# A hybrid decoder layer: x read in order of time and permuted out of PSUM, the constants read first, B and C turned on TensorE, states permuted back by ScalarE

## The chip, the core and the metric

The kernel runs on one core of one Trainium2 chip. The metric is the device time of one execution in microseconds (us), less is better. The kernel before took 3020.07 us, the median of three runs (3012.84 to 3021.89). The profiled execution is a fourth one and took 3016.45 us.

The engines are TensorE (PE; PEld are its weight loads), VectorE (DVE), ScalarE (ACT), GpSimd (POOL) and SyncE (SP). SP computes nothing here: its queue issues every DMA, in one order. Each engine works through its own queue in the order in which the program was built, and waits at an instruction until the semaphores that it names are there.

## What is computed

One layer over 2048 tokens of 1024 channels, all in float32:

```
h    = rmsnorm(x, norm_mix);  u, z, xbc, dt = split(h @ w_in)
y_a  = s5(u)      # 64 groups of 16 channels, each a complex diagonal
                  # state of 64:  s[t] = abar * s[t-1] + Bbar u[t]
                  # y = Re(C s) + d * u, then gelu and a gate
y_b  = mamba2(z, conv4(xbc), dt)       # 16 heads, chunks of 128
x    = x + concat(rmsnorm(y_a), rmsnorm(y_b)) @ w_out
out  = rmsnorm(x + swiglu_ffn(rmsnorm(x)))
```

S5 takes eight steps of time at once. With 256 such blocks, u of a group is a matrix of 128 rows (8 steps j by 16 channels) and 256 columns. A table M1 turns a block into what it adds to the state, the scan runs over the blocks, and two tables M2 and Q give the output: `y = M2' u + Q' state`. All three are made on the chip from lambda, the step, B and C.

## The kernel before

**Projection.** x is read in blocks of 512 tokens (four chunks of 128). `load_block` reads a chunk, squares it on ACT for the norm's sum, computes the scale on DVE and multiplies. `transposed_split` transposes the block on TensorE, 128 by 128, into PSUM tiles `ps_t`, and splits each into a rounded high part (ACT) and a rest (DVE). `project_pairs` takes two tiles of 128 output columns at a time: `split_w` reads the weights (`wst`), rounds them on ACT (`whi`), takes the rest on POOL (`wlo`), and each half block of 512 tokens then needs 24 matmuls into `ps_in` (lines 81 to 83). The first half of the tokens goes through u, then the convolved columns, then z; of the second half, two u tiles are made before the scan, and the rest beside it and after it. The convolution runs on DVE (`acc`, three products a tile).

**Order of time.** The columns that S5 and the convolution want are not in order of time. Token t of a chunk is `8*c + j`, and they want j outermost, c inside. `rows` does this in the load of x: it reads eight sets of sixteen rows, each row eight tokens after the one before. The projected columns then come out as (chunk k, j, c). What is written at the end goes back through `rows`.

**The start.** SP's queue holds the four chunks of block 0, then the constants `cm` (identity, triangles), eight small vectors, two weight tiles, and block 1. `s5_tables` then reads lambda, B with its states on the partitions (pieces of 16 elements), and C in tiles `ct` of 128 rows, eight of which are transposed on TensorE (`ps_c`) for each of two arrangements; seven DMAs from `zt` fill the upper part of M2's table with zeros. For each of eight sets of groups DVE makes W and Q (`W`, six products), TensorE transposes W (`ps_m`) and computes `ps_k`.

**The scan.** `s5_inputs` computes `ps_x` for eight groups and ACT copies it into X, as (block's m, s). `s5_scan` runs 15 steps of four DVE operations over m, a scan over the 16 s, and then adds the carried states to X with products `f1` and `f2` (two buffers under one tag `f`). The result XG lies as (m, s), and the matmul `ps_y` with Q reads it with a step of 16 elements, as (s, m).

**The other mixer.** `ssd_pair` handles two heads in 64 columns each; its product `ps_yd` takes the four chunks of the first head, then those of the second.

**What sets the order.** The program is written without semaphores. A scheduler with a model of time puts each engine's instructions in order, and ends of tiles in pools set when buffers come free: five slots of 16 KB (`take`, `slot`), two buffers for `wst`, `whi` and `wlo`, two for the conv's `xp`, one for `acc`. `issue_after` holds instructions behind a given one.

Of the kernel before, what the change touches and what calls it, by code (L numbers as in the profile page):

```python
# [112 lines left out]
def transposed_split(k, xb, gcol, hi, lo, wide=None):  # L113
# [16 lines left out]
    for kk in range(KD):  # L130
# [7 lines left out]
        k.evac = nc.scalar.activation(hi[:, kk, :], ps, AF.Identity, scale=g)  # L138
        nc.vector.scalar_tensor_tensor(lo[:, kk, :], ps, g, hi[:, kk, :].bitcast(F32), op0=MUL, op1=SUB)
# [132 lines left out]
def s5_tables(k, sp):  # L272
# [145 lines left out]
    for dst, (u0, u1) in ((c1_, (k.c_re, k.c_im)), (c2_, (k.c_im, k.c_re))):  # L418
        ct = sp.tile([P, 8, P], F32, name="ct", tag="M1", bufs=1)
        nc.sync.dma_start(ct[:, :, 0:64], u0.rearrange("(t a) h p -> (a h) t p", a=8))  # L420
        nc.sync.dma_start(ct[:, :, 64:128], u1.rearrange("(t a) h p -> (a h) t p", a=8))
        for q in range(2):
            ps = k.ps_x.tile([P, 512], F32, tag="x", name="ps_c")
# [1105 lines left out]
```

## Time and profile before

| | us |
|---|---|
| median of three runs | 3020.07 |
| the profiled execution | 3016.45 |
| its span on the core | 3014.7 |
| first projection matmul (L81) | 28.86 |
| first `ps_dt` matmul, which follows the u projection | 157.93 |
| first `ps_x` matmul of the scan | 454.66 |
| first `ps_w` matmul of the output projection | 1286.85 |

A window gives the busy time of each engine between two times, and the clock that TensorE was granted (1.00 is full). A wait gives who stood still and for whose result; a row of the timeline gives start, length, engine, line, operation, output and inputs. Matmul records overlap, so that the pace of a run of them is its length divided by their number, not the length of one record. A float32 matmul that is not rounded to fp32r counts as two records.

### The profile page before, as it was taken

To read this page: it belongs to the slowest core of one execution; us is meant where nothing else is said; L and a number is where in the kernel's file an instruction comes from. 1 tells how busy PE (TensorE), PEld (TensorE's weight loads), DVE (VectorE), ACT (ScalarE), POOL (GpSimd) and SP (SyncE) were. 2 spreads that over 40 slices of the span, in tenths; PEclk is the share of its full clock that TensorE was granted. 3 is DMA by queue.
4 is the path that set the end of the run, shared out by engine and by line. 5 is a ranking of instruction groups with operands and counts; after the bars stand their busy time and mean duration, and the time that the engine had idled before them with its cause. 6 is when DMAs were issued, how large, how long until landed. Compare 5 with 4: busy or idle time off the path is not lost.

```text
span 3014.7 us, 35741 instructions
## 1 busy us (share of the span) xinstructions
PE 2833.0 (94%) x12972; PEld 2257.6 (75%) x12972; DVE 2102.2 (70%) x3953; ACT 1118.2 (37%) x1817; POOL 535.6 (18%) x462
## 2 busy tenths in 40 slices
PE   4898999999999989989899999999999999999996
PEld 3776777677787777768677788887788887878875
DVE  5586218989668888797878755556655557677686
ACT  3134322333454333332434433334333334243343
POOL 1343311114366766510000000000000000000000
PEclk8999999999999999999999999999999999999998
DMA  6455335443446454545455222233222224545444
GB/s 118 116 157 169 117 97 173 140 140 104 132 129 191 145 165 140 174 153 172 134 167 161 74 75 82 84 112 101 96 84 84 79 76 141 194 168 192 165 153 140
DMA packets 331992, 398.84 MB, mean 132 GB/s; under 512 B 49804, under 2 KB 249592, under 8 KB 331816
## 3 DMA queue, kind: packets, MB, share of 16 engines
q1 hardware_dynamic: 331816, 396.56, 42.1%
q8 instruction: 102, 1.67, 0.2%
q14 instruction: 74, 0.61, 0.1%
HBM read 264.39 MB, written 132.12 MB: 132 GB/s over the span
## 4 chain that ended last, share of the span: by engine, by line
PE 62%; DVE 19%; DMA 11%; issue 3%; ACT 2%; SPq 2%; POOL 1%; DVEq 0%; ACTq 0%; POOLq 0%
PE ps_w L1126 40%; PE ps_in L81 4%; PE ps_in L83 4%; PE ps_in L82 4%; DMA s<-ybD 2%; DVE s L947 2%; DVE acc L731 1%; DMA out_dram<-x 1%; PE ps_y L575 1%; DVE wS L947 1%; PE ps_glu L81 1%; PE ps_glu L82 1%; PE ps_glu L83 1%; DVE x L1132 1%; DVE s L1179 1%
## 5 line engine op out<-in xcount | busy, mean ns | idle before, releaser
L1126 PE MATMUL ps_w<-s,wS 128*128 128x512 f32 x3936 | 957.7, 397 | 39.0 <-DVE s L947 16.8
L1126 PEld LDWEIGHTS ps_w<-s,wS 128*128 128x128 f32 x3936 | 747.3, 191 | 213.9 <-DVE s L947 18.8
L1126 PE MATMUL ps_w<-s,wA 128*128 128x512 f32 x2952 | 731.4, 398 | 29.8 <-DVE x L1132 10.3
L1126 PEld LDWEIGHTS ps_w<-s,wA 128*128 128x128 f32 x2952 | 558.8, 190 | 167.7 <-DVE x L1132 12.1
L81 PE MATMUL ps_in<-s,whi 128*128 128x512 f32 x896 | 353.5, 395 | 9.1 <-ACT xp L718 9.0
L83 PE MATMUL ps_in<-s,wlo 128*128 128x512 f32 x896 | 351.8, 395 | 1.6 <-POOL wlo L69 1.6
L82 PE MATMUL ps_in<-s,whi 128*128 128x512 f32 x896 | 352.9, 394 | 0.0
L942 ACT CAST wS<-sum 128x512 fp32r<-128x512 f32 (+1 forms) x336 | 203.5, 611 | 396.7 <-PE ps_w L1126 195.6
L947 DVE TENSOR_TENSOR wS<-sum,wS 128x512 fp32r<-128x512 f32 (+1 forms) x336 | 225.5, 675 | 140.5 <-ACT wS L942 139.9
L69 POOL TENSOR_TENSOR wlo<-wst,whi 128x1024 fp32r<-128x1024 f32 x72 | 188.7, 2621 | 424.1 <-ACT whi L66 424.0
L942 ACT CAST wA<-s 128x512 fp32r<-128x512 f32 (+1 forms) x252 | 150.7, 610 | 242.0 <-PE ps_w L1126 162.1
L81 PEld LDWEIGHTS ps_in<-s,whi 128*128 128x128 f32 x896 | 169.4, 189 | 49.0 <-ACT xp L718 10.3
L83 PEld LDWEIGHTS ps_in<-s,wlo 128*128 128x128 f32 x896 | 169.4, 189 | 40.9 <-issue 3.1
L82 PEld LDWEIGHTS ps_in<-s,whi 128*128 128x128 f32 x896 | 169.4, 189 | 36.9 <-issue 2.3
L1132 DVE TENSOR_TENSOR gu<-ps_w,gu 128x512 f32<-128x512 f32 x134 | 92.5, 691 | 148.3 <-PE ps_w L1126 144.5
L803 POOL TENSOR_TENSOR s<-cm,dtas 128x512 fp32r<-128x512 f32 x128 | 161.8, 1292 | 76.0 <-PE ps_seg L804 76.0
L947 DVE TENSOR_TENSOR wA<-s,wA 128x512 fp32r<-128x512 f32 (+1 forms) x252 | 165.1, 671 | 3.2 <-ACT wA L942 3.2
L1132 DVE TENSOR_TENSOR x<-ps_w,x 128x512 f32<-128x512 f32 x160 | 108.7, 685 | 57.1 <-PE ps_w L1126 56.9
L731 DVE SCALAR_TENSOR_TENSOR acc<-xp,cols,acc 128x1024 f32<-128x1024 f32 x72 | 102.7, 1426 | 50.6 <-ACT acc L729 49.9
L66 ACT CAST whi<-wst 128x1024 fp32r<-128x1024 f32 x72 | 75.5, 1049 | 167.9 <-PE ps_in L82 99.8
L1137 ACT COPY gu<-ps_w 128x512 f32<-128x512 f32 x134 | 78.4, 586 | 141.7 <-PE ps_w L1126 141.4
L1139 DVE TENSOR_TENSOR x<-x,sg 128x512 f32<-128x512 f32 x125 | 85.0, 686 | 65.7 <-ACT sg L1137 38.5
(354 smaller groups left out, 3612.8 us busy)
## 6 DMA issues: line engine op xcount, KB each, us to landing
wst<-in_w_in_dram SPq DMA_DIRECT2D x56, 512.0 KB
s<-in_w_gate_dram SPq DMA_DIRECT2D x22, 1024.0 KB
s<-in_w_up_dram SPq DMA_DIRECT2D x22, 1024.0 KB
actD<-gu SPq DMA_DIRECT2D x44, 512.0 KB
s<-actD SPq DMA_DIRECT2D x16, 1024.0 KB
xD<-xo SPq DMA_DIRECT2D x24, 512.0 KB
uD<-ev SPq DMA_DIRECT2D x16, 512.0 KB
zD<-sz SPq DMA_DIRECT2D x32, 256.0 KB
```

Source lines behind the costliest of these rows:

```text
L69: eng.tensor_sub(lo, st, hi.bitcast(F32))
L81: nc.tensor.matmul(ps, wh[:, i, :], rh[:, i, :], start=(i == 0), stop=False)
L82: nc.tensor.matmul(ps, wh[:, i, :], rl[:, i, :], start=False, stop=False)
L83: last = nc.tensor.matmul(ps, wl[:, i, :], rh[:, i, :], start=False, stop=(i == n - 1))
L731: V.scalar_tensor_tensor(acc, tap(i), col(i), acc, op0=MUL, op1=ADD)
L803: G.tensor_mul(r, bc(k.tri.unsqueeze(1), [P, 4, P]), bc(part, [P, 4, P]))
L942: a = k.nc.scalar.copy(op[:, 0], raw)
L947: b = eng.tensor_sub(op[:, 1, part], raw[:, part], op[:, 0, part].bitcast(F32))
L1126: nc.tensor.matmul(ps, a[:, p, i, :], b[:, q, i, :], start=(root == name and i == 0 and p + q == 0), stop=(i == n - 1 and p == 1), skip_gr ...
L1132: V.tensor_add(dst, ps, dst if onto else src)
L1137: nc.scalar.copy(dst, bank[root])
L1139: V.tensor_add(block, block, dst)
```

## The change

There are six parts.

1. x of blocks 0 to 3 is read row by row. The permutation moves to the two operations that take `ps_t` out of PSUM: they read each eighth element. A block's columns are now (j, n) with 64 n, so that whoever takes `ps_in` out reads (j, k, c) and writes (k, j, c) as before (`chunks`, `by_chunk`).
2. `cm` is read first. The load of block 1 is issued after the first two weight tiles (`early`), and the second of these is no longer held behind the evacuation of block 0.
3. B and C are read raw, with the groups on 64 partitions, into slot 3, in six DMAs (B in rows of 4 KB, C in pieces of 256 B); `by_state` turns them with 64 transposes of 64 rows and eight ACT copies. Slot 3 held block 1 of x before.
4. The scan's last addition stays in f1, on all 128 partitions (before: two additions over 64 partitions each, straight into XG). ACT copies f1 into XG, four times a set, now as (s, m), so that the matmul with Q reads adjacent elements.
5. `ps_yd` alternates between the two heads.
6. The outputs of u are written as 8 runs of 64 instead of runs of 16.

```diff
@@ transposed_split
-        k.evac = nc.scalar.activation(hi[:, kk, :], ps, AF.Identity, scale=g)
-        nc.vector.scalar_tensor_tensor(lo[:, kk, :], ps, g, hi[:, kk, :].bitcast(F32), op0=MUL, op1=SUB)
+        view = lambda t: t[:, kk, :].rearrange("p (j n) -> p j n", j=8)
+        src = ps.rearrange("p (n j) -> p j n", j=8)
+        k.evac = nc.scalar.activation(view(hi), src, AF.Identity, scale=g)
+        nc.vector.scalar_tensor_tensor(view(lo), src, g, view(hi).bitcast(F32), op0=MUL, op1=SUB)
@@ fetch_block (new; load_block calls it or is given xb)
+        k.load = k.nc.sync.dma_start(xb[:, i, :], k.x[ch * P : ch * P + P, :])
@@ project_pairs
-            with k.tc.issue_after(behind) if behind and pair else nullcontext():
-                w = split_w(k, k.w_in[:, c0 : c0 + P], lo_pool=True)
+            w = split_w(k, k.w_in[:, c0 : c0 + P], lo_pool=True)
             pair.append((w, start(half)))
-        behind = None
+        if i == 0 and early:
+            early()
@@ s5_tables
+    raw = k.take(3, [P, 3 * 16 * 64], F32)
+    b_raw = raw[0:64].rearrange("g (x h) -> g h x", h=16)
+    c_raw = raw[64:128].rearrange("g (h x) -> g h x", h=16)
+    for i, (u, v) in enumerate(((k.b_re, k.c_re), (k.b_im, k.c_im), (k.b_re, k.c_re))):
+        nc.sync.dma_start(raw[0:64, i * 1024 : i * 1024 + 1024], u.rearrange("g p h -> g (p h)"))
+        nc.sync.dma_start(c_raw[:, :, i * 64 : i * 64 + 64], v)
...
-        nc.sync.dma_start(bt[0:64], u0.rearrange("g p h -> p g h"))
-        nc.sync.dma_start(bt[64:128], u1.rearrange("g p h -> p g h"))
+    def by_state(dst, part, i):
+        g = slice(part * 64, part * 64 + 64)
+        src = (b_raw, c_raw)[part][:, :, i * 64 : i * 64 + 128]
+        for q in range(2):
+            ps = k.ps_x.tile([P, 512], F32, tag="x", name="ps_c")
+            for a in range(8):
+                nc.tensor.transpose(ps[:, a * 64 : a * 64 + 64], src[:, q * 8 + a], k.ident[g, g])
+            nc.scalar.copy(dst[:, :, q * 8 : q * 8 + 8], ps.rearrange("p (h g) -> p g h", g=64))
+    by_state(b1, 0, 0)
+    by_state(b2, 0, 1)
...
-                nc.tensor.transpose(ps[:, tt * P : tt * P + P], ct[:, q * 4 + tt, :], k.ident)
-            nc.scalar.copy(dst[:, q * 32 : q * 32 + 32, :].rearrange("p a h -> p (a h)"), ps)
+    by_state(c1_, 1, 0)
+    by_state(c2_, 1, 1)
@@ s5_scan
+        V.tensor_add(f1, f1, X[:, :, ri, 0:15, :])
         for g2 in range(2):
             src = slice(g2 * 64, g2 * 64 + 64)
-            xg = XG[dst, :, g2, 16:256].rearrange("p a (m s) -> p a m s", s=16)
-            V.tensor_add(xg, f1[src], X[src, :, ri, 0:15, :])
-            nc.scalar.copy(XG[dst, :, g2, 0:16], CY[src, :, ri, :])
+            xg = XG[ri * 64 : ri * 64 + 64, :, g2, :].rearrange("p a (s m) -> p a s m", m=16)
+            nc.scalar.copy(xg[:, :, :, 1:16].rearrange("p a s m -> p a m s"), f1[src])
+            nc.scalar.copy(xg[:, :, :, 0], CY[src, :, ri, :])
...
-            nc.tensor.matmul(ps[:, g2, :], Q[:, g, :], XG[:, a, g2, :].rearrange("p (m s) -> p s m", s=16), start=False, stop=True)
+            nc.tensor.matmul(ps[:, g2, :], Q[:, g, :], XG[:, a, g2, :], start=False, stop=True)
@@ ssd_pair
-    for hh, L in enumerate(Ls):
-        for i in range(4):
+    for i in range(4):
+        for hh, L in enumerate(Ls):
@@ trunk_kernel
-    xb0 = load_block(k, 0, k.slot)
     nc.sync.dma_start(cm, ins["c_mat"])
+    xb0 = fetch_block(k, 0, k.slot)
+    load_block(k, 0, k.slot, xb0)
```

How the queues move is seen at three places. The first is SP's queue from B and C on, ahead of the first writes of u. Before (`b_` and `ct` are B and C, `zt` the zeros, `wst` a weight tile, `uD` the store of u):

```order
L287 DMA ls<-in_s_log_step_dram 64x1
L406 DMA b_1094<-in_s_b_re_dram 64x64x16
L407 DMA b_1094<-in_s_b_im_dram 64x64x16
L406 DMA b_1095<-in_s_b_im_dram 64x64x16
L407 DMA b_1095<-in_s_b_re_dram 64x64x16
L420 DMA ct<-in_s_c_re_dram 128x8x64
L421 DMA ct<-in_s_c_im_dram 128x8x64
L432 DMA m2D<-zt 1024x1x16
```

After, from the last of the seven zero fills on (`s_850` is slot 3 with the raw B and C):

```order
L461 DMA m2D<-zt 1024x1x112
L312 DMA s_850<-in_s_b_re_dram 64x1024
L313 DMA s_850<-in_s_c_re_dram 64x16x64
L312 DMA s_850<-in_s_b_im_dram 64x1024
L313 DMA s_850<-in_s_c_im_dram 64x16x64
L312 DMA s_850<-in_s_b_re_dram 64x1024
L313 DMA s_850<-in_s_c_re_dram 64x16x64
L249 DMA uD<-ev 1024x1x128
```

B and C moved from ahead of the zero fill to behind it; the fourth weight tile stands among the zero fills now.

The second place is TensorE's queue at the end of the first u projection. Before (`ps_m` and `ps_k` belong to the first set of tables, `ps_dt` to the next stage):

```order
L83 MATMUL ps_in<-s_335,wlo 128x512
L452 MATMUL ps_m_1157<-cm,W 128x128 x4
L452 MATMUL ps_m_1163<-cm,W 128x128 x4
L472 MATMUL ps_k<-W,BD 32x128 x8
L658 MATMUL ps_dt<-s_163,wdA 32x512
```

After (`ps_c` are the transposes of the raw B and C):

```order
L82 MATMUL ps_in<-s_336,whi 128x512
L83 MATMUL ps_in<-s_335,wlo 128x512
L439 MATMUL ps_c<-cm,s_850 128x64 x36
L687 MATMUL ps_dt<-s_163,wdA 32x512
L688 MATMUL ps_dt<-s_164,wdB 32x512
```

Of the 64 transposes, twelve stand after the first pair of u tiles (48 matmuls of block 1), 36 here, and 16 among the ps_dt. The first tables come later: 53 matmuls of the next projection stand ahead of the first ps_m, and 731 instead of 628 projection matmuls ahead of the last.

The third place is DVE's queue at the end of a set's scan. Before (`t_` and X belong to the next set's scan, which is laced in):

```order
L561 TENSOR_TENSOR f_3467<-f_3467,f_3468 128x960
L533 TENSOR_TENSOR t_3680<-t_3680,X 128x128
L566 TENSOR_TENSOR XG<-f_3467,X 64x4x240 x2
L559 TENSOR_TENSOR f_3476<-CY,A_155 128x960
L534 TENSOR_TENSOR X<-t_3680,t_3681 128x8x16
L560 TENSOR_TENSOR f_3477<-CY,A_154 128x960
```

After:

```order
L590 TENSOR_TENSOR f_3520<-f_3520,f_3521 128x960
L562 TENSOR_TENSOR t_3735<-t_3735,X 128x128
L591 TENSOR_TENSOR f_3520<-f_3520,X 128x960
L588 TENSOR_TENSOR f_3530<-CY,A_155 128x960
L563 TENSOR_TENSOR X<-t_3735,t_3736 128x8x16
L560 TENSOR_TENSOR t_3735<-X,CA 128x128
L561 TENSOR_TENSOR t_3736<-X,CI 128x128
L562 TENSOR_TENSOR t_3735<-t_3735,X 128x128
L589 TENSOR_TENSOR f_3531<-CY,A_154 128x960
```

One addition stands where two were, and three more steps of the next scan stand ahead of the second product; f_3531 takes the buffer of f_3520, which ACT's copies read. Between the first ps_x and the last ps_y, 867 projection matmuls stand in TensorE's queue, before 962; the 95 others stand behind. From the output projection on, the queues of SP and ACT are the same.

More of the change, by code (lines that the diff above doesn't have):

```diff
@@ L160, in transposed, with fetch_block @@
                 nc.vector.tensor_scalar(dst[:, i, :], ps, g, None, MUL)
-def load_block(k, blk, pool):
-    nc = k.nc
+def fetch_block(k, blk, pool):
     xb = pool([P, 4, D], F32)
@@ L168, in load_block @@
         ch = blk * 4 + i
-        k.load = nc.sync.dma_start(xb[:, i, :], rows(k.x, ch))
+        k.load = k.nc.sync.dma_start(xb[:, i, :], k.x[ch * P : ch * P + P, :])
+    return xb
+def load_block(k, blk, pool, xb=None):
+    nc = k.nc
+    if xb is None:
+        xb = fetch_block(k, blk, pool)
+    for i in range(4):
+        ch = blk * 4 + i
         junk = k.cp.tile([P, D], BF16, tag="junk", name="junk", bufs=1)
@@ L185, in split_block, with project, project_pairs @@
     return hi, lo
-def project(k, half, h, tiles, second=None, behind=None):
-    for _ in project_pairs(k, half, h, tiles, second, behind):
+def project(k, half, h, tiles, second=None, early=None):
+    for _ in project_pairs(k, half, h, tiles, second, early):
         pass
-def project_pairs(k, half, h, tiles, second=None, behind=None):
+def project_pairs(k, half, h, tiles, second=None, early=None):
     n = len(tiles)
@@ L216, in project_pairs, with chunks, by_chunk @@
         yield
+def chunks(ps):
+    return ps.rearrange("p (j k c) -> p k j c", j=8, c=16)
+def by_chunk(t):
+    return t.rearrange("p (k j c) -> p k j c", j=8, c=16)
 def tile_u(k, m):
@@ L242, in evac @@
             sz = k.up.tile([P, 512], F32, tag="sz", name="sz", bufs=2)
-            nc.scalar.activation(sz, ps, AF.Silu)
+            nc.scalar.activation(by_chunk(sz), chunks(ps), AF.Silu)
             nc.sync.dma_start(k.zD[m * P : (m + 1) * P, (half * 2 + b) * 512 : (half * 2 + b + 1) * 512], sz)
@@ L417, in s5_tables @@
     V.tensor_sub(B2, B2, tb)
[L418 to L423, printed above, removed]
-            for tt in range(4):
-                nc.tensor.transpose(ps[:, tt * P : tt * P + P], ct[:, q * 4 + tt, :], k.ident)
-            nc.scalar.copy(dst[:, q * 32 : q * 32 + 32, :].rearrange("p a h -> p (a h)"), ps)
+    by_state(c1_, 1, 0)
+    by_state(c2_, 1, 1)
     G.tensor_scalar(c1_[64:128], c1_[64:128], -1.0, None, MUL)
@@ L659, in ssd_dt @@
             nc.tensor.matmul(ps[0:32, :], k.wdB[:, i, :], rl[:, i, :], start=False, stop=(i == KD - 1))
[L660 removed]
+        nc.scalar.copy(by_chunk(dtc[:, b * 512 : b * 512 + 512]), chunks(ps[0:32, :]))
     pt = k.ps_g.tile([P, 8, 32], F32, tag="g", name="ps_dtT")
@@ L717, in evac @@
         def evac(b, ps):
-            nc.scalar.copy(xp[:, b * 4 : b * 4 + 4, 3:11, :], ps.rearrange("p (k j c) -> p k j c", j=8, c=16))
+            nc.scalar.copy(xp[:, b * 4 : b * 4 + 4, 3:11, :], chunks(ps))
         def finish():
@@ L814, in ssd_pair @@
     pyd = k.ps_x.tile([P, 4, P], F32, tag="x", name="ps_yd")
-    for hh, L in enumerate(Ls):
-        for i in range(4):
+    for i in range(4):
+        for hh, L in enumerate(Ls):
             nc.tensor.matmul(pyd[hh * 64 : hh * 64 + 64, i, :], xdt[:, i, hh, :], L[:, i, :], start=True, stop=True)
@@ L1431, in trunk_kernel, with early @@
             nc.scalar.mul(k.cols[:, C_BGLU : C_BGLU + 8], k.cols[:, C_BGLU : C_BGLU + 8], 0.5)
+        def early():
+            k.xb1 = fetch_block(k, 1, k.slot)
         def second():
             with tc.issue_after(evac.ins):
-                xb = load_block(k, 1, k.slot)
+                xb = load_block(k, 1, k.slot, k.xb1)
             return split_block(k, xb, C_NM, k.slot)
-        project(k, 0, h, us, second, evac.ins)
+        project(k, 0, h, us, second, early)
         first = [i.ins for i in (k.load, k.scaled, k.evac, k.turned)]
```

6 lines of the change are left out of this document (1 added, 5 removed).

## The prediction

> **What bounds the kernel now.** I read the page's busy times first, then the windows by stage, then the waits of TensorE in the first 100 us.
>
> ```profile
> PE 2833.0 (94%) x12972; PEld 2257.6 (75%) x12972; DVE 2102.2 (70%) x3953; ACT 1118.2 (37%) x1817; POOL 535.6 (18%) x462
> ```
>
> TensorE is busy 94% of the span. The idle 182 us and TensorE's own work are what can shrink. In the windows (columns: stretch, length, busy us of PE, PEld, DVE, ACT, POOL, granted clock, DMA share, GB/s) they lie as follows:
>
> ```profile
> 0.00:50.00 50.00, 18.78 (x87) 14.79 (x87) 16.67 (x58) 18.14 (x30) 5.84 (x11) 0.95 0.58 127
> 50.00:100.00 50.00, 31.75 (x133) 26.18 (x134) 39.84 (x153) 11.67 (x19) 17.22 (x18) 0.74 0.78 130
> 100.00:157.00 57.00, 57.00 (x256) 47.25 (x255) 22.90 (x57) 11.23 (x16) 20.86 (x32) 1.00 0.35 98
> 157.00:250.00 93.00, 90.59 (x530) 69.19 (x529) 88.87 (x96) 34.35 (x55) 44.84 (x44) 1.00 0.58 172
> 250.00:300.00 50.00, 41.14 (x168) 32.83 (x167) 27.82 (x63) 22.90 (x33) 11.04 (x15) 0.93 0.54 154
> 475.00:808.00 333.00, 326.89 (x1408) 238.22 (x1407) 304.43 (x707) 120.82 (x182) 80.26 (x66) 1.00 0.43 134
> 808.00:1285.00 477.00, 451.28 (x2555) 365.62 (x2553) 370.49 (x658) 196.84 (x299) 306.70 (x242) 0.97 0.52 159
> 1285.00:3014.00 1729.00, 1646.16 (x7058) 1328.16 (x7058) 1188.67 (x2084) 648.84 (x1111) 9.81 (x2) 0.98 0.38 125
> ```
>
> Four readings. The first 100 us hold 49.5 us of TensorE idle, with the clock down to 0.74. From 157 to 250, while the S5 tables are made, DVE and PE are both near full. The S5 scan (475 to 808) has PE at 98% and DVE at 91%: either can set its length. From 1285 on the change touches nothing. The waits name the start's culprits (us in total, times, longest):
>
> ```profile
> PE ps_t L120 <- DMA cm<-in_c_mat_dram: 21.5, 1, 21.5
> PE ps_c L425 <- DMA ct<-in_s_c_re_dram: 9.8, 1, 9.8
> PE ps_t L120 <- DVE s L176: 8.1, 4, 5.6
> PE ps_c L425 <- DMA ct<-in_s_c_im_dram: 6.3, 1, 6.3
> ```
>
> The identity matrix (in cm) sits behind four loads of x; block 1 of x is late (the 8.1); and two waits are for C, in TensorE's queue ahead of projection matmuls that were ready.
>
> **The start, part by part.** The timeline gives the pace of x, the first and second group of projection matmuls, the zero fill, the resumption after the last C, and the end of the u projection:
>
> ```profile
> DMA  0003455555589446345554555453555455554551
> 7.63 1.06 ACT L171 ACTIVATE junk<-s 128x1024 bf16<-128x1024 f32 x1 [5.62 <-DMA s<-in_x_dram]
> 20.99 1.06 ACT L171 ACTIVATE junk<-s 128x1024 bf16<-128x1024 f32 x1 [3.22 <-DMA s<-in_x_dram]
> 24.35 1.42 DVE L176 TENSOR_SCALAR s<-s,inv 128x1024 f32<-128x1024 f32 x2
> 27.40 5.36 DVE L139 SCALAR_TENSOR_TENSOR s<-ps_t,cols,s 128x512 fp32r<-128x512 f32 x8 [1.46 <-ACT s L138]
> 28.86 0.50 PE L81 MATMUL ps_in<-s,whi 128*128 128x512 f32 x1
> 61.00 13.27 SPq L432 DMA_DIRECT2D m2D<-zt  x7
> 66.68 0.78 PE L81 MATMUL ps_in<-s,whi 128*128 128x512 f32 x1
> 89.55 1.94 PE ps_c L425 x8
> 91.14 0.78 PE L83 MATMUL ps_in<-s,wlo 128*128 128x512 f32 x1
> 156.37 1.04 PE L452 MATMUL ps_m<-cm,W 128*128 128x128 f32 x8
> 157.34 0.66 PE L472 MATMUL ps_k<-W,BD 128*32 128x128 f32 x16
> 157.93 0.42 PE L658 MATMUL ps_dt<-s,wdA 128*32 128x512 f32 x1
> 73.18 0.45 PE ps_in L82 x2
> ```
>
> *First matmul.* Four 512 KB loads of x arrive from 7.63 to 20.99, so 4.45 us each; the DMA strip of 0.5 to 21 us shows about half of the engines busy. The old source starts with a dimension of 8 rows, the new one is plain rows. If all engines work, a load takes 2.2 us: data flows from 3.2 (7.63 less 4.45), cm takes 1.1 of it, four loads 8.9, so the last lands at 13.2. From the last landing to the first projection matmul it is 28.86 less 20.99, 7.9 us: 21.1. The earlier cm lets half of the transposes go sooner; I take 20, a gain of 9. Bounds: 12 if even the latency shrinks; minus 1 if x stays at half width, since cm's 1.1 us then comes on top.
>
> *Block 1.* A projection matmul is 0.227 us (two in 0.45), so the first group of 48 took 28.86 to 39.8, and the second group began at 66.68: 26.8 between them. Now block 1 lands 4.4 (two weights) plus 8.9 after block 0, at 26.5. Square, norm and scaling took 4.8 of the 7.9 us above (20.99 to 25.77): 31.3. The first group ends at 20 plus 10.9, 30.9. Eight evacuations at DVE's pace (5.4 us) and the small transposes of lambda make the second group start near 38: 7 between. Gain 19.8; without full width block 1 is some 18 us later and this goes too.
>
> *B and C.* The second wait (9.8 us up to 89.55, and 1.6 of transposes until 91.14) goes, but there are 64 transposes of 64 rows instead of 16. At 0.12 us each (eight from 156.37 until ps_k starts at 157.34) that is 7.7 us, 12 of them amid the second pair and 52 later. What is late next is the raw load: SP issues it behind the zero fill, 13.3 us of issuing, and slot 3 is free only at 37, after block 1's transposes. TensorE asks for it at 38 plus 10.9, 48.9; I put its landing at 50 to 51: a wait of 2, bounds 0 and 9 (the old wait for c_re).
>
> Sum: 20 + 384 x 0.227 + 7 + 2 + 7.7 = 124 for the end of the u projection, against 157.9. 1.6 us of early table work in the old 157.9 only moves: gain **32**.
>
> *What gives part of it back.* In the old order DVE made B's products and the first tables while TensorE was behind, then waited 27.1 us for it:
>
> ```profile
> DVE W L445 <- PE ps_m L452: 27.1, 1, 27.1
> L445 DVE TENSOR_TENSOR W<-B,RV 128x1024 f32<-128x1024 f32 x8 | 10.0, 1252 | 42.5 <-PE ps_m L452 27.1 <-POOL RV L373 15.4
> L460 DVE TENSOR_TENSOR W<-cc,PW 128x1152 f32<-128x1152 f32 x8 | 13.0, 1619 | 0.3 <-DMA qD<-W 0.2
> ```
>
> Now B and most of C are turned after the u projection, so six products (7.5 us) and the first group (three of 1.25 and three of about 1.45, 8.1) fall into the stretch where DVE is busy 88.9 of 93. Up to 15.6 us of the 32 return as waits of TensorE for ps_m; I take 12 (the conv work has some slack). The loads of blocks 2 and 3 at full width save some of the 8.9 us idle in 250 to 300: 5. Arrival at the scan: **25 earlier**, bounds 5 and 37.
>
> **The scan and what follows.**
>
> ```profile
> 504.72 1.72 PE ps_y L575 x4
> 519.44 1.73 PE ps_y L574 x8
> 470.30 3.67 PE ps_x L505 x32
> 858.32 1.51 PE ps_yd L817 x16
> L566 DVE TENSOR_TENSOR XG<-f,X 64x960 f32<-64x960 f32 x32 | 41.0, 1282 | 0.7
> L561 DVE TENSOR_TENSOR f<-f,f 128x960 f32<-128x960 f32 x16 | 20.7, 1296 | 0.0
> L731 DVE SCALAR_TENSOR_TENSOR acc<-xp,cols,acc 128x1024 f32<-128x1024 f32 x30 | 41.2, 1372 | 14.0 <-ACT acc L729 13.9
> L66 ACT CAST whi<-wst 128x1024 fp32r<-128x1024 f32 x20 | 21.0, 1051 | 49.9 <-PE ps_in L82 26.8 <-DMA wst<-in_w_in_dram 15.0 <-issue 8.0
> L506 ACT COPY X<-ps_x 128x512 f32<-128x512 f32 x32 | 18.6, 587 | 41.1 <-DVE XG L566 26.4 <-PE ps_x L505 14.6
> L718 ACT COPY xp<-ps_in 128x512 f32<-128x512 f32 x22 | 12.7, 577 | 9.0 <-PE ps_in L83 9.0
> ```
>
> L575 reads XG with a step of 16 elements: 0.43 us a record, L574 with adjacent elements 0.216. There are 128 records: TensorE saves 27.4 us. On DVE 32 adds over 64 partitions (41.0) become 16 over 128 (L561's 1.30 each, 20.7): 20 saved. ACT takes 32 copies of 960 elements, at L66's rate 0.98 us each, 32 us; its 121 busy of 333 hide them, unless its order does not (below). The order also puts 95 projection matmuls (21.6 us) and two conv tiles (six of L731, 8.2 us DVE) behind the scan. So PE's 326.9 become 277.9 and DVE's 304.4 become 276. At PE's old idle of 6 us the stretch takes 284; with DVE's old idle of 28.6 it takes 305. I take 300, nearer to DVE's since the scan is its chain: 33 less.
>
> After it the 21.6 us are added. The ps_yd matmuls alternate between the two halves of the columns: 16 records took 1.51, and L505, which alternates already, needs 0.115 for 256 columns against 0.216 of L574, so for 128 columns 0.058, 0.92 for 16. Over 32 pairs that is 19, bounds 0 and 19; I take 15, as DVE and POOL end some waits there. Net **7 lost**.
>
> Sum against the profiled execution: 3016.45 - 25 - 33 + 7 = **2965**. That execution lies 3.6 under the median of the runs shown; I predict 2966.
>
> **Reads with a step, a rule against the change.** The evacuations of ps_t now read PSUM with a step of 8 elements, and XG is written with a step of 16. L506 reads PSUM with a step of 16 in 587 ns, L718 in runs of 16 in 577: ACT pays nothing. For DVE from PSUM no row has such a step; L506 is the nearest, so I take 0 (bound: twice L139's 0.67 us). The Trainium skill, "Advanced Engine Details and Errata", section "Memory Cachelines", says that accesses each falling on another line (16 bytes in SBUF, 8 in PSUM) are penalised. The trace agrees for TensorE (0.43 against 0.216) and not for ACT (587 against 577).
>
> **Rivals.**
> *ACT as the new link (slower).* The scan's f tiles have two buffers, so the second f2 product waits for ACT's copies of the first f1, which in ACT's queue stand behind casts of weights, which wait for TensorE (26.8 over 20 casts, 1.34 each). Queued behind that product is the rest of DVE's scan. A wait costs two copies (1.96), a cast with its wait (2.4) and an evacuation (0.58), 4.9, less an add and a product on DVE (2.6) and a few small ones: about 1, partly in the slack above. If the cover failed, 16 x 4.9 = 78: **3043**. It decides from 51/16 = 3.2 us a wait. Against it: ACT is idle 64% there. Chance 0.06.
> *DVE keeps the scan and tables, TensorE's savings become idle.* Start 10 (the 15.6 and more returned), scan 28, ps_yd nothing, so 21.6 lost: 3016 - 10 - 28 + 22 = **3000**. For it: DVE 91 and 96% busy. Chance 0.22.
> *x stays at half width.* The change doesn't do what it says of x: the first two gains vanish and only the C waits go, 11.4 less 7.7 of transposes and some of that to the tables: 3016 - 3 - 33 + 7 = **2987**. Chance 0.10.
> *Strided access is slow on ACT and DVE.* 32 evacuations, each 0.67 more on DVE, and 32 copies 0.98 more: 21 and, half hidden, 16: 2966 + 37 = **3003**; this is what the rule above would make of it. Chance 0.07.
> *All of it is realised.* 37 + 49 - 3: **2933**. Chance 0.13.
> *The forecast*, 2966 with 2950 to 2982: 0.42.
>
> The range 2928 to 3004 leaves out the slow case, half of the 3003 and the tails of 3000 and 2933: 0.18. A difference of 0.3% (9 us) is about what can be told from none. Faster by more: all but the slow case and the tails of the 3000s, 0.88; within: 0.06; slower: 0.06.
>
> **What will show it.** Right: first L81 near 20; the DMA strip at 0.9 during x; ps_dt near 125; ps_y's Q matmuls at 0.22 a record; 16 ps_yd in about 0.9. Wrong: PE waiting for the raw B and C over 9 us, DVE waiting in the scan for ACT, x loads still 4.4 us apart, evacuations of ps_t over 1 us, or idle in the scan above 40 us.

## The result, and the profile after

The changed kernel takes **2948.8 us** (median of 4 runs, 2946.7 to 2953.3), the kernel before 3019.0 (3012.8 to 3021.9): ratio 0.977, 95% interval 0.975 to 0.978. That is 70 us less; 54 were forecast. One run of a later kernel, of 6771 us where its three others took 2979 to 2981, is left out below.

To see where the 70 us come from, cut both executions at the same events: the first ps_dt (end of the u projection), the first ps_x (arrival at the scan), the last ps_y, the first ps_w, the end. The first ps_w of before starts at 1280.6, and not at the 1286.85 of the table ahead of the prediction. The windows of before (stretch, length, busy us of PE, PEld, DVE, ACT, POOL with the number of instructions, clock, DMA share, GB/s):

```profile
0.00:157.90 157.90, 108.43 (x492) 88.79 (x492) 79.87 (x269) 41.94 (x67) 44.32 (x62) 0.90 0.57 118
157.90:454.70 296.80, 281.19 (x1361) 223.49 (x1357) 145.84 (x186) 104.44 (x152) 94.53 (x91) 0.99 0.45 136
454.70:807.50 352.80, 345.45 (x1515) 251.24 (x1515) 316.86 (x759) 126.12 (x192) 80.26 (x66) 1.00 0.43 134
807.50:1280.60 473.10, 451.02 (x2553) 365.57 (x2551) 366.59 (x652) 193.88 (x295) 304.03 (x241) 0.97 0.52 158
1280.60:3014.70 1734.10, 1646.91 (x7060) 1328.48 (x7060) 1193.07 (x2090) 651.81 (x1115) 12.49 (x3) 0.98 0.38 126
```

and of the changed kernel:

```profile
0.00:122.80 122.80, 105.62 (x500) 86.29 (x500) 61.76 (x256) 41.94 (x66) 34.52 (x55) 0.99 0.57 144
122.80:413.60 290.80, 281.71 (x1397) 224.89 (x1395) 166.94 (x199) 106.08 (x156) 118.72 (x98) 0.99 0.45 140
413.60:738.60 325.00, 304.96 (x1420) 234.83 (x1420) 290.26 (x737) 175.35 (x213) 69.50 (x56) 0.98 0.45 139
738.60:1213.00 474.40, 452.63 (x2647) 365.21 (x2646) 378.06 (x660) 204.83 (x308) 316.87 (x251) 0.98 0.54 163
1213.00:2947.20 1734.20, 1652.54 (x7062) 1333.18 (x7060) 1190.39 (x2088) 649.42 (x1114) 10.60 (x3) 0.97 0.38 125
```

| stage | before | after | difference | forecast |
|---|---|---|---|---|
| start to first ps_dt | 157.9 | 122.8 | -35.1 | -32 |
| tables, to first ps_x | 296.8 | 290.8 | -6.0 | +7 |
| scan, to last ps_y | 352.8 | 325.0 | -27.8 | -33 |
| to first ps_w | 473.1 | 474.4 | +1.3 | +7 |
| rest | 1734.1 | 1734.2 | +0.1 | 0 |
| sum | | | -67.5 | -51 |

**The start** came to the time worked out for it. The strip of the DMA engines (forty equal slices of that stretch, each digit the busy share in tenths) between 0.5 and 21 us (before: about half busy), the two groups of projection matmuls and the first ps_dt in the timeline of after, and TensorE's waits up to there:

```profile
DMA  0049999999999992000125999999999999999999
18.92 0.51 PE L81 MATMUL ps_in<-s,whi 128*128 128x512 f32 x1
37.51 0.50 PE L81 MATMUL ps_in<-s,whi 128*128 128x512 f32 x1
122.83 0.41 PE L687 MATMUL ps_dt<-s,wdA 128*32 128x512 f32 x1
PE ps_t L120 <- DVE s L187: 11.2, 1, 11.2
PE ps_c L439 <- DMA s<-in_s_b_im_dram: 2.2, 1, 2.2
```

**The tables**: TensorE's waits between ps_dt and ps_x, two rows of before and then the one of after:

```profile
PE ps_in L81 <- ACT xp L718: 9.0, 3, 5.9
PE ps_m L452 <- DVE W L447: 2.4, 2, 1.5
PE ps_k L501 <- DVE W L491: 6.6, 4, 2.4
```

DVE has 21 us more to do in that stage than before (166.9 against 145.8), as forecast, yet only 4.2 us of it come back as waits for W (6.6 against 2.4), and the 9.0 us are gone.

**The scan**: groups of after (line, operation, shapes, count, then busy us and mean ns, then the idle time ahead and what ended it), and DVE's waits there:

```profile
L595 ACT COPY XG<-f 64x960 f32<-64x960 f32 x32 | 59.3, 1853 | 52.3 <-DVE f L591 52.0
L604 PE MATMUL ps_y<-XG,Q 128*128 128x256 f32 x128 | 39.9, 427 | 14.6 <-ACT XG L595 14.6
L591 DVE TENSOR_TENSOR f<-f,X 128x960 f32<-128x960 f32 x16 | 22.6, 1413 | 0.0
L760 DVE SCALAR_TENSOR_TENSOR acc<-xp,cols,acc 128x1024 f32<-128x1024 f32 x24 | 33.0, 1376 | 5.3 <-ACT acc L758 5.2
DVE t L560 <- ACT X L535: 22.1, 1, 22.1
DVE f L589 <- ACT XG L595: 12.9, 7, 2.4
DVE acc L760 <- ACT acc L758: 5.2, 2, 3.4
```

Read them together with the windows. DVE's busy time fell by 26.6 us: 18.4 on the adds (41.0 to 22.6) and 8.2 on conv tiles that moved out (41.2 to 33.0). The scan fell by 27.8. TensorE's fell by 40.5 (345.5 to 305.0), and its idle time there grew from 7.4 to 20.0, most of it waiting for XG (14.6). So the scan's gain follows DVE's and not TensorE's: DVE's 290.3 and its waits (22.1, 12.9, 5.2) make 330 of a stretch of 325, before 316.9 and 22.2, 13.9, 4.5 make 357 of 353 (some records overlap). And ACT's copies cost twice what was put down for them.

**Behind the scan** the ps_yd matmuls keep TensorE busy 16.6 us less (groups of before and of after):

```profile
L817 PE MATMUL ps_yd<-L,xdt 128*64 128x128 f32 x512 | 52.9, 288 | 0.0
L846 PE MATMUL ps_yd<-L,xdt 128*64 128x128 f32 x512 | 36.3, 284 | 0.0
```

### The profile page after: what moved, and what is told of

The parts are those of the page before. It is cut to its first block, busy times and chain, and to the rows that moved or that the text cites. A ratio compares the mean times of both kernels' runs of the same rounds, so it can differ in the third digit from the quotient of the medians.

```text
span 2947.2 us, 35852 instructions
## 1 busy us (share of the span) xinstructions
PE 2797.5 (95%) x13020; PEld 2244.4 (76%) x13020; DVE 2087.4 (71%) x3937; ACT 1177.6 (40%) x1853; POOL 550.2 (19%) x462
## 4 chain that ended last, share of the span: by engine, by line
PE 41%; DVE 10%; DMA 6%; issue 1%; ACT 0%; SPq 0%; DVEq 0%; ACTq 0%
PE ps_w L1155 40%; DMA s<-ybD 2%; DVE s L976 2%; DMA out_dram<-x 1%; DVE x L1161 1%; DVE s L1208 1%; DMA s<-actD 1%; DVE s L1014 1%; DVE wS L976 1%; DVE wA L976 1%; DMA x<-x3D 1%; DVE x L1168 1%; DVE x L1367 0%; DMA x<-xaD 0%; DVE sum L1115 0%
## 5 line engine op out<-in xcount | busy, mean ns | idle before, releaser
L69 POOL TENSOR_TENSOR wlo<-wst,whi 128x1024 fp32r<-128x1024 f32 x72 | 183.9, 2555 | 371.2 <-ACT whi L66 344.8
L760 DVE SCALAR_TENSOR_TENSOR acc<-xp,cols,acc 128x1024 f32<-128x1024 f32 x72 | 109.4, 1519 | 26.6 <-ACT acc L758 26.0
```

The source lines that it names most:

```text
L69: eng.tensor_sub(lo, st, hi.bitcast(F32))
L760: V.scalar_tensor_tensor(acc, tap(i), col(i), acc, op0=MUL, op1=ADD)
```

## The experiments

Unless said otherwise each is the changed kernel (2948.8) with one edit. The kernel before ran beside each group, at 3016.6 to 3018.1.

### Four parts, each undone

**The order of the ps_yd matmuls.**

```diff
-    for i in range(4):
-        for hh, L in enumerate(Ls):
+    for hh, L in enumerate(Ls):
+        for i in range(4):
```

> The changed kernel with the ps_yd matmuls in their old order (all of one half of the columns, then all of the other). Theory: the stretch from the first ps_seg to the first ps_w is TensorE's, so the 16.6 us that ps_yd saved there (52.9 to 36.3 us busy) come back nearly whole: 13 to 17 us slower than the changed kernel. Rival: DVE and POOL set that stretch, and TensorE's saving became idle: 0 to 5 us slower.

Measured: 2968.7 (2967.0 to 2972.2), 20 slower. The stretch from the last ps_y to the first ps_w:

```profile
739.30:1226.50 487.20, 467.62 (x2649) 380.32 (x2647) 375.68 (x658) 204.81 (x307) 313.86 (x251) 0.98 0.53 158
```

12.8 us longer (474.4), with TensorE 15.0 busier: TensorE sets it, and the rival falls. The other 7 us lie behind the first ps_w, where the edit touches nothing (1741 us against 1734; the fourteen profiles have 1730 to 1741 there); they are not explained.

**The end of a set's scan.**

```diff
-        V.tensor_add(f1, f1, X[:, :, ri, 0:15, :])
...
-            nc.scalar.copy(xg[:, :, :, 1:16].rearrange("p a s m -> p a m s"), f1[src])
...
+            xg = XG[dst, :, g2, 16:256].rearrange("p a (m s) -> p a m s", s=16)
+            V.tensor_add(xg, f1[src], X[src, :, ri, 0:15, :])
...
-            nc.tensor.matmul(ps[:, g2, :], Q[:, g, :], XG[:, a, g2, :], start=False, stop=True)
+            nc.tensor.matmul(ps[:, g2, :], Q[:, g, :], XG[:, a, g2, :].rearrange("p (m s) -> p s m", s=16), start=False, stop=True)
```

> The changed kernel with the old end of a set's scan: 32 DVE adds over 64 partitions into XG, Q read with a step of 16, no copies of f by ACT. The order then has 962 instead of 867 projection matmuls between the first ps_x and the last ps_y. Theory: TensorE does the 95 matmuls (21.6 us) in either place, so what the scan change is worth is the 21.9 us saved on the Q matmuls less the 12.6 us by which TensorE's idle grew in the scan: 9 us slower than the changed kernel. Rival 1: the whole 27.8 us by which the scan became shorter are lost: 25 to 30 us slower. Rival 2: the waits for ACT eat all of it: within 3 us of the changed kernel.

Measured: 2969.9 (2965.6 to 2973.1), 21 slower; none of the three. The windows of the scan and of the stretch behind it:

```profile
413.60:766.20 352.60, 347.22 (x1514) 253.38 (x1514) 317.33 (x759) 125.95 (x192) 80.55 (x66) 0.99 0.44 134
766.20:1233.30 467.10, 433.38 (x2553) 345.28 (x2552) 369.86 (x654) 194.35 (x296) 309.82 (x241) 0.98 0.53 161
```

The scan is 27.6 longer, as rival 1 has it, but with the 95 matmuls back in the scan the stretch behind shrinks by only 7.3 us and not by 21.6: TensorE is idle 33.7 us there without them, 21.8 with them. In the changed kernel some two thirds of the moved matmuls' 21.6 us fill time that TensorE would have spent waiting. That is what I had wrong.

**The view in which x is loaded**, and the evacuations with it; cm stays first.

```diff
-        k.load = k.nc.sync.dma_start(xb[:, i, :], k.x[ch * P : ch * P + P, :])
+        k.load = k.nc.sync.dma_start(xb[:, i, :], rows(k.x, ch))
```

> The changed kernel with x loaded by its old view (8 rows as the first dimension), and the evacuations that go with it; cm stays first. Theory: a 512 KB load takes 4.45 us again, the first projection matmul starts at 27 to 29 us (18.9 now), the second group near 57 (37.5 now), the last conv tile's wait of 9 us at 250 to 300 returns: 25 to 32 us slower. Rival 1: the tables on DVE set the arrival at the scan, and the start's loss is hidden in part: about 10 us slower. Rival 2: cm ahead of x is what brought the start's gain, not x's order: 5 us slower or less, with the first projection matmul at 20 to 22.

Measured: 2996.2 (2991.0 to 3001.7), 47 slower, more than any of the three. The scan begins at 456.7, as late as in the kernel before (454.7): without the order of x the other parts gain nothing up to there, and cm first alone brings none (first projection matmul at 30.6, before 28.9; the second group at 70.4, where near 57 was expected). What I had not counted is in the second stage, in the waits of TensorE and of ACT:

```profile
PE ps_in L81 <- ACT whi L66: 16.7, 1, 16.7
ACT junk L180 <- DMA xb<-in_x_dram: 23.4, 8, 4.7
```

The eight squares of blocks 2 and 3 stand in ACT's queue and wait for x; behind them stands the cast of a weight, and behind that TensorE. In the changed kernel ACT waits 1.6 us there.

**B and C**, loaded by state as before.

```diff
-    by_state(b1, 0, 0)
-    by_state(b2, 0, 1)
+    for bt, (u0, u1) in ((b1, (k.b_re, k.b_im)), (b2, (k.b_im, k.b_re))):
+        nc.sync.dma_start(bt[0:64], u0.rearrange("g p h -> p g h"))
...
```

> The changed kernel with B and C loaded by state as before (16 transposes of C ahead of the projection, no raw copy); x stays in order of time. Theory 1: the loads of C, with their short rows, land late whatever x does, so with the second group of 48 matmuls now done at 48 us TensorE waits 15 to 35 us for them, and most of it is lost: 12 to 25 us slower; the change of B and C is what lets x's gain through. Theory 2 (the forecast's sizes): the wait of 11.4 us comes back and 7.7 us of transposes go, and DVE gets B earlier: between 3 us faster and 4 us slower.

Measured: 2959.9 (2955.3 to 2963.2), 11 slower, between the two. TensorE's waits in the start:

```profile
PE ps_c L446 <- DMA ct<-in_s_c_re_dram: 7.6, 1, 7.6
PE ps_c L446 <- DMA ct<-in_s_c_im_dram: 5.9, 1, 5.9
```

13.5 us (2.2 in the changed kernel) put the first ps_dt at 135.9 instead of 122.8. DVE then has 21 us less to do at the tables and gives 7.7 back, so the scan begins 5.4 later; the rest of the 11 lies behind the scan, outside the edit. The turning of B and C is worth 5 us of the arrival at the scan, x's order 43 (each with the other in place). Of theory 1 the mechanism holds, at less than its price.

The four losses add to some 100 us, 29 more than the change gains. In the four profiles 14 us of them lie behind the first ps_w, which no edit touches. For the rest, two of them may lean on each other: the scan's change moves 95 matmuls behind the scan, and the cheaper ps_yd makes room for them. That is argued; no run undid both.

### The scan's copies, four ways

**Read with the step, written in a row.**

```diff
-            nc.scalar.copy(xg[:, :, :, 1:16].rearrange("p a s m -> p a m s"), f1[src])
+            nc.scalar.copy(xg[:, :, :, 1:16], f1[src].rearrange("p a m s -> p a s m"))
```

> The changed kernel, whose 32 copies of f into XG by ACT walk the other way round: they read f with a step of 16 elements and write XG in runs of 15 (in the changed kernel they read f in a row and write with a step of 16, 1.85 us each). Theory: ACT pays for the step on the written side; a copy takes 0.95 to 1.1 us, the 14.6 us for which TensorE waits for XG shrink to 4 or less, and the kernel is 7 to 12 us faster than the changed one. Rival: any step costs, read or written; a copy stays at 1.7 to 2.0 us and the time within 3 us of the changed kernel.

**No step on ACT, the step on TensorE.**

```diff
-            nc.scalar.copy(xg[:, :, :, 1:16].rearrange("p a s m -> p a m s"), f1[src])
...
+            nc.scalar.copy(XG[dst, :, g2, 16:256].rearrange("p a (m s) -> p a m s", s=16), f1[src])
...
-            nc.tensor.matmul(ps[:, g2, :], Q[:, g, :], XG[:, a, g2, :], start=False, stop=True)
+            nc.tensor.matmul(ps[:, g2, :], Q[:, g, :], XG[:, a, g2, :].rearrange("p (m s) -> p s m", s=16), start=False, stop=True)
```

> The changed kernel with XG left in order of chunks: ACT copies f in a row on both sides, TensorE reads XG with a step of 16 again; DVE's part is as in the changed kernel (16 adds over 128 partitions). Theory: a copy takes 0.95 to 1.0 us, a Q matmul 0.43 us a record; TensorE has 27 us more to do in the scan, of which some 12 fit where it waited for ACT: 12 to 18 us slower than the changed kernel. Rival: DVE's saving on the adds is what made the scan shorter, not Q's step: within 4 us of the changed kernel.

**The step on DVE's add** (into the buffer of f2), ACT copies in a row.

```diff
-        V.tensor_add(f1, f1, X[:, :, ri, 0:15, :])
...
+        V.tensor_add(fp.rearrange("p a s m -> p a m s"), f1, X[:, :, ri, 0:15, :])
...
-            nc.scalar.copy(xg[:, :, :, 1:16].rearrange("p a s m -> p a m s"), f1[src])
+            nc.scalar.copy(xg[:, :, :, 1:16], fp[src])
```

> The changed kernel, where DVE's add of X writes its sum already in order of time (with a step of 15 elements, into the buffer of f2), and ACT's copies read and write in rows of 15. The order has 853 instead of 867 projection matmuls in the scan. Theory: DVE pays nothing for the step (the add stays at 1.35 to 1.45 us) and ACT's copy takes 0.95 to 1.1 us: 7 to 12 us faster than the changed kernel. Rival: DVE pays for a written step as ACT does, the add takes 2.0 us or more, 10 us and more of DVE in the scan: no faster than the changed kernel.

**DVE writes XG itself**, with the step, in 32 adds.

```diff
-        V.tensor_add(f1, f1, X[:, :, ri, 0:15, :])
...
-            nc.scalar.copy(xg[:, :, :, 1:16].rearrange("p a s m -> p a m s"), f1[src])
+            V.tensor_add(xg[:, :, :, 1:16].rearrange("p a s m -> p a m s"), f1[src], X[src, :, ri, 0:15, :])
```

> The changed kernel without ACT's copies: DVE adds X and writes XG in order of time itself, 32 adds over 64 partitions, with a step of 16 elements; TensorE reads Q's operand in a row. The order has 962 projection matmuls in the scan, as the kernel before. Theory: if DVE pays nothing for the step, an add takes 1.28 us as in the kernel before, and the scan is TensorE's: 352.8 less some 25, 325 to 332 us with all 962, against 325 with 867, so 6 to 15 us faster than the changed kernel, since 95 matmuls less stand behind the scan. Rival: the written step costs DVE as it costs ACT, an add takes 2 us or more, DVE has 23 us more, and the kernel is 5 to 20 us slower than the changed one.

The groups that carry the step or lost it, one of the first kernel, then two of the second with the window of its scan, two of the third, one of the fourth:

```profile
L595 ACT COPY XG<-f 64x960 f32<-64x960 f32 x32 | 60.3, 1885 | 50.9 <-DVE f L591 50.5
L595 ACT COPY XG<-f 64x960 f32<-64x960 f32 x32 | 31.8, 995 | 26.4 <-DVE f L591 26.0
L604 PE MATMUL ps_y<-XG,Q 128*128 128x256 f32 x128 | 61.7, 603 | 0.1
414.10:737.00 322.90, 322.63 (x1420) 233.59 (x1420) 289.12 (x737) 148.82 (x214) 72.26 (x57) 1.00 0.46 141
L596 ACT COPY XG<-f 64x960 f32<-64x960 f32 x32 | 31.8, 995 | 61.9 <-DVE f L592 61.6
L592 DVE TENSOR_TENSOR f<-f,X 128x960 f32<-128x960 f32 x16 | 29.9, 1868 | 0.0
L594 DVE TENSOR_TENSOR XG<-f,X 64x960 f32<-64x960 f32 x32 | 63.7, 1991 | 0.7
```

| who pays the step | time | against 2948.8 | judgement |
|---|---|---|---|
| ACT, reading | 2950.4 (2949.2 to 2951.3) | +2 | rival: a copy takes 1.89 us, read or written alike |
| TensorE, reading | 2946.9 (2944.2 to 2952.6) | -2 | rival: nothing is lost |
| DVE, writing its sum | 2947.1 (2945.4 to 2948.0) | -2 | near the rival's price (1.87 for 1.41 us in the mean), no gain |
| DVE, writing XG | 2979.9 (2978.5 to 2981.1, 3 runs) | +31 | rival, and more than its 5 to 20 |

The second is the one to dwell on. With the step back on TensorE its Q matmuls are as dear as before the change, TensorE is busy 322.6 of 322.9 us, and the kernel is as fast as the changed one. **Moving the step from TensorE to ACT, the largest saving that the forecast counts on TensorE (27.4 us), was worth nothing**, because the same step on ACT made DVE and TensorE wait for XG; the version without the step, further down, bears this out. The scan of 323 to 325 us has two lids at almost one height: TensorE with the step, and DVE with ACT's copies without it.

### Moved matmuls without the saving

The kernel with the old end of the scan (2969.9), where the last conv tiles' matmuls are queued behind the last set's ps_y.

```diff
+            if a == 1 and g2 == 1:
+                k.late = mm.ins
...
-            gemm_cm(k, ps, w, h[b])
+            n_gemm += 1
+            with k.tc.issue_after(k.late) if n_gemm > late else nullcontext():
+                gemm_cm(k, ps, w, h[b])
```

> The second of these kernels (the old end of a set's scan: 32 DVE adds, Q read with a step) with one thing more: the projection matmuls of the last three and a half conv tiles are queued behind the ps_y of the last set, so that 861 instead of 962 projection matmuls stand in the scan (867 in the changed kernel). Theory: what the change of the scan was worth is where those matmuls stand: TensorE had 347 of 352.6 us to do there, and has 23 us less now; the stretch from the first ps_x to the last ps_y falls to 326 to 335 us, the one after the scan grows by 7 to 11, and the kernel comes within 8 us of the changed one (2949 to 2957), with neither of the scan's two savings. Rival: DVE with its old adds (317 us busy and its waits) holds the scan at 343 to 352 us, and the matmuls behind it are added: 2965 to 2980.

Measured: 2977.6 (2974.3 to 2979.5); the rival. The window of the scan, and the idle time of Q's matmuls in the groups of the whole run:

```profile
415.50:761.00 345.50, 323.02 (x1413) 233.24 (x1413) 305.18 (x753) 118.91 (x183) 67.15 (x57) 0.98 0.43 132
L607 PE MATMUL ps_y<-XG,Q 128*128 128x256 f32 x128 | 61.9, 605 | 19.1 <-issue 18.8 <-DVE XG L598 0.3
```

TensorE has 24 us less to do than with all 962, but the scan loses only 7: TensorE runs out of matmuls and stands 18.8 us ahead of the last set's Q. The row names no releaser, but DVE's last four adds run from 745.15 on, and the first Q starts at 752.21, as the third of them ends. So moving the matmuls alone is not enough, and DVE's shorter adds are needed. What these bring with all 962 matmuls in the scan was not run.

### A version without the step

If neither TensorE, ACT nor DVE is to pay, the reordering must be done where a step is free. The evacuations of ps_t are such a place. Before they read PSUM in a row, after with a step of 8 elements:

```profile
L138 ACT ACTIVATE s<-ps_t,cols 128x512 fp32r<-128x512 f32 x32 | 20.4, 692 | 7.0 <-PE ps_t L120 7.0
L139 DVE SCALAR_TENSOR_TENSOR s<-ps_t,cols,s 128x512 fp32r<-128x512 f32 x32 | 22.4, 745 | 90.2 <-ACT s L138 89.8
L140 ACT ACTIVATE s<-ps_t,cols 128x512 fp32r<-128x512 f32 x32 | 20.4, 692 | 3.2 <-PE ps_t L120 3.0
L141 DVE SCALAR_TENSOR_TENSOR s<-ps_t,cols,s 128x512 fp32r<-128x512 f32 x32 | 22.4, 745 | 88.5 <-ACT s L140 88.5
```

So u, XG and ps_y are kept in an order with runs of 8 elements, and ACT puts the result in order of time when it reads ps_y.

```diff
-            nc.scalar.copy(ev[:, :, b * 64 : b * 64 + 64], ps.rearrange("p (j n) -> p j n", j=8))
+            nc.scalar.copy(ev.rearrange("p j (m s) -> p j m s", s=8)[:, :, :, b * 4 : b * 4 + 4], ps.rearrange("p (j q m) -> p j m q", j=8, m=16))
...
+        for h in range(2):
+            nc.scalar.copy(X[:, a, :, :, h * 8 : h * 8 + 8], ps[:, :, h * P : h * P + P].rearrange("p r (m s) -> p r m s", s=8))
...
+            for h in range(2):
+                xg = XG[ri * 64 : ri * 64 + 64, :, g2, h * P : h * P + P].rearrange("p a (m s) -> p a m s", s=8)
+                nc.scalar.copy(xg[:, :, 1:16], f1[src, :, :, h * 8 : h * 8 + 8])
...
-        nc.scalar.activation(yg, ps, AF.Gelu_apprx_tanh)
+        yv = yg.rearrange("p g (h s m) -> p (g h) s m", h=2, m=16)
+        nc.scalar.activation(yv, ps.rearrange("p g (h m s) -> p (g h) s m", h=2, m=16), AF.Gelu_apprx_tanh)
```

> A version drawn from these runs: the changed kernel, where u, XG and ps_y stand in an order of time within half, step in the chunk, chunk (runs of 8), so that TensorE reads everything in a row, the reordering is done where ACT reads PSUM, and ACT's copies of f write runs of 8 elements (64 of 480 elements instead of 32 of 960; the copies of X are split in two as well). Theory: a step costs ACT nothing on PSUM and nothing in runs of 8; a copy of 480 elements takes 0.55 to 0.65 us, TensorE's waits for XG fall from 14.6 us to 5 or less, and it is 5 to 12 us faster than the changed kernel. Rival 1: a run of 8 elements costs as single ones do, 0.95 us a copy and more: within 4 us. Rival 2: the scan is held by DVE's chain and the waits for X, not by XG: within 4 us, with the waits for XG gone.

Measured: **2939.0** (2935.7 to 2941.6, 5 runs), ratio to the kernel before 0.974 (0.972 to 0.975): 10 us better than the changed kernel. The copies, the scan's window, and two waits there, TensorE's and DVE's:

```profile
L597 ACT COPY XG<-f 64x480 f32<-64x480 f32 x64 | 34.7, 589 | 37.1 <-DVE f L592 36.8
414.00:725.60 311.60, 299.62 (x1419) 233.10 (x1419) 289.83 (x737) 157.43 (x309) 65.81 (x56) 0.99 0.47 145
PE ps_y L606 <- ACT XG L597: 5.9, 2, 4.3
DVE f L590 <- ACT XG L597: 0.9, 1, 0.9
```

The theory holds: runs of 8 cost next to nothing (64 copies of 480 elements keep ACT busy for 34.7 us, 32 copies of 960 in a row took 31.8), DVE's wait of 12.9 for XG is 0.9, and the scan is 13.4 us shorter with DVE's work unchanged.

### DVE and POOL

What is left on DVE? In the timeline of the changed kernel its long instructions coincide with POOL's L69, the low parts of the weights. One POOL row, and DVE's at that time:

```profile
476.60 2.46 POOL L69 TENSOR_TENSOR wlo<-wst,whi 128x1024 fp32r<-128x1024 f32 x1 [18.77 <-ACT whi L66]
476.71 2.50 DVE L561 TENSOR_TENSOR t<-X,CI 128x128 f32<-128x128 f32 x1
```

L561 takes 0.28 us otherwise (median). Two kernels on the 2939.0 version move L69 of the second half of x to DVE; the first also holds back the conv tiles as above.

```diff
-            w = split_w(k, k.w_in[:, c0 : c0 + P], lo_pool=True)
+            w = split_w(k, k.w_in[:, c0 : c0 + P], lo_pool=half == 0)
```

> The version with everything in a row for TensorE, where in the second half of x the low parts of the weights (L69) are made by DVE instead of POOL, and the last three and a half conv tiles are queued behind the last ps_y, so that 863 projection matmuls stand in the scan (867 without it). In the trace of that version each of the 18 L69 on POOL in the scan (2.37 us and more) goes with one DVE instruction that takes 2.3 to 3.4 us where its like take 0.28 to 1.15: DVE stands still while POOL works, some 2.1 us each, 39 in all. Theory: that is so, and DVE makes the low part in 1.2 to 1.3 us: DVE's chain in the scan is 15 to 17 us shorter, TensorE with 299.6 us of work becomes the bound, the scan takes 301 to 306 us (311.6 now), and the kernel 2929 to 2935 (2939). Rival: the long DVE instructions are not POOL's doing, or DVE needs as long for the low part (2.4 us): the scan takes 311 to 325 us and the kernel is no faster than 2939.

> The same, with the low parts on DVE, but without holding conv tiles back: the order then has 1011 projection matmuls between the first ps_x and the last ps_y (867 in the changed kernel), 144 more (32.7 us). Theory: TensorE bounds the scan, 332 to 340 us; behind it only a third to a half of the 32.7 us is won, 461 to 467 us (477.5), since DVE, ACT and POOL set much of that stretch; in all 2945 to 2960, slower than with the tiles held back. Rival: where the matmuls stand is of no account, and it is within 4 us of the kernel with the tiles held back.

Measured: 2965.7 (2956.9 to 2973.3) with tiles held back, 2943.5 (2943.1 to 2945.6) without. For the first the scan's window, the group of L69, DVE's largest wait and TensorE's; then the two windows of the second:

```profile
411.50:741.80 330.30, 299.88 (x1416) 233.45 (x1416) 271.60 (x755) 161.08 (x311) 21.80 (x39) 0.96 0.45 139
L69 DVE TENSOR_TENSOR wlo<-wst,whi 128x1024 fp32r<-128x1024 f32 x18 | 22.0, 1224 | 19.3 <-ACT whi L66 19.2
PE ps_y L609 <- ACT XG L600: 22.3, 1, 22.3
413.30:752.60 339.30, 332.12 (x1565) 260.64 (x1564) 282.29 (x765) 173.16 (x325) 29.90 (x50) 0.99 0.46 143
752.60:1212.20 459.60, 426.46 (x2507) 338.43 (x2505) 370.82 (x656) 191.29 (x293) 296.52 (x233) 0.97 0.54 162
```

The price was right: DVE makes a low part in 1.22 us, and though it took over 22.0 us of work its busy time fell by 18.2 (289.8 to 271.6), so some 40 us of its 290 had been standing still for POOL. The gain was not: L69 now waits in DVE's queue for ACT's cast (19.2 us), which the POOL version did not make DVE do, and at the end TensorE has nothing left and waits 22.3 us in one piece. The scan is 19 us longer, not 6 to 11 shorter; another 13 us lie behind it (490.1 against 477.5) and are not explained. Without the hold the order fills the scan with 1011 matmuls, TensorE is the bound at 339.3 (332 to 340 expected), and 17.9 of the 32.7 us come back behind the scan, a little more than expected. Both expectations of where to put the matmuls fall: this one is 22 us faster than with tiles held back, not slower and not the same. It is 4.5 slower than 2939.0, which is not clear of noise (ratios to the kernel before of 0.974 to 0.977 and 0.972 to 0.975). A version with the low parts on DVE behind casts that are done in time was not tried.

## Why the prediction was right

The time lay in the range, and the sign was right. It lies 1 us below the 2950 to 2982 of the likeliest case, though, 17 us from its 2966 and 16 from the 2933 at which everything is realised: the likeliest case named the right places and was 16 to 17 us too cautious. By stage it missed more: the arrival at the scan came 16 us earlier than forecast, the scan gained 5 less, the stretch behind it lost 6 less. It is luck that the last two cancel. (Its last step, from 2965 to 2966, leaves out most of the 3.6 us that it names; with them it is 2969.) Step by step:

- **First matmul** at 20: 18.9, in part by luck. The last load of block 0 was there by 9.70, when ACT squares it, and not at 13.2; but 9.2 us followed and not 7.9, as DVE was still scaling the first two chunks, and two casts of weights stood ahead of ACT's first evacuation, before one. **Block 1**, a gap of 7: the first group ends 48 x 0.227 after 18.92, at 29.8, the second starts at 37.5, 7.7. **Raw B and C**, a wait of 2: 2.2. **End of the u projection** at 124: 122.8. Its sum counts all 64 transposes, 7.7 us; by the order shown 48 stand ahead of the first ps_dt, and 36 of them took 3.0 us (119.86 to 122.83), so it is some 4 us, and other gaps fill the difference. The loads went at the strip of 0.9 that was asked for.
- **What gives part of it back**: this term was mis-sized. 12 us of waits at the tables were put down, and 5 us saved at blocks 2 and 3; the trace shows 4.2 and 9.0. The arrival at the scan came 41 us earlier, not 25: as much as the whole miss. DVE's extra work was there (21 us), but I priced it as TensorE's waiting, though the order that I showed has 731 instead of 628 projection matmuls ahead of the last ps_m, 23 us of other work for TensorE. That this order covers the waits is argued from the two traces; no run took it away.
- **The scan**, 33: 27.8. The forecast had 305 with DVE's old idle, 284 with TensorE's, and took 300 for what was 333 long; 28 less is the 305, so it was DVE's. Its terms held (adds 20.3 forecast, 18.4 measured; conv 8.2 both). TensorE's 27.4 showed in its busy time (21.9) and not in the end, as the kernel with Q's step put back shows. To that extent the rival in which TensorE's savings become idle came true, in the scan alone.
- **ACT's 32 copies at 0.98**: 1.85. "ACT pays nothing" was read off rows that read PSUM and carried over to a write in SBUF. Copies with no step took 0.995, so the row for the price was right and the step was the error. The rival of slow steps was thus half true: on ACT's copies (0.86 more, 0.98 put down), not on the evacuations (745 against 745 ns). It put 16 us on the copies; the version without the step wins back 10.
- **ACT as the new link**: the mechanism came, small, and with it one of the signs of being wrong, DVE waiting in the scan for ACT. DVE's second f2 product waited 12.9 us in 7 times, and TensorE 14.6 for XG; nowhere near 78. The sign for Q came as well: its records start 0.22 us apart, before 0.43.
- **After the scan**, +7: +1.3. ps_yd gave 16.6 of 19, and undoing it showed that TensorE has the use of it. The rival in which it gives nothing falls.
- **x stays at half width** falls by the strip.

## What to carry to other kernels

Where two engines have nearly the same height in a stage, count a saving on one of them only up to the other's height, and ask what the operation that makes it possible does to the second. A reordering is worth trying where the data passes PSUM anyway: here it cost nothing there, and the same step in SBUF nearly doubled ACT's copy (0.995 to 1.85 us). And before pricing a delay on one engine as a wait of another, look in the order for what the other has to do meanwhile.
